# Half of the softmax tiles of an attention block transposed by VectorE and a DRAM round trip, with all engines in source order

## The chip, the core and the metric

The kernel runs on one core of a Trainium2 chip. Five engines work beside each other, each in its own instruction order: TensorE (PE, matmuls; weight loads are listed apart as PEld), VectorE (DVE), ScalarE (ACT), GpSimd (POOL) and SyncE (SP), whose work here is to issue transfers. ScalarE issues transfers too. The metric is the device time of one execution in microseconds, as the median of several runs.

## What is computed

One encoder layer for 512 positions of width 2048. The parts that matter here:

```python
h = rms_norm(x) * (1 + scale) + shift            # scale, shift, gate from silu(c) @ w_cond
aq, ak, av, ag, gq, gk, gv, gg, lr_f, lr_b = split(h @ w_in)
for window, dilation in ((128, 1), (512, 4), (2048, 16)):     # 16 heads x 64
    s = q @ k.T / 8 + bias(relative position);  mask outside the dilated window
    o_p, lse_p = softmax(s) @ v, logsumexp(s)
att = sum_p softmax_p(lse_p) * o_p
a_out = att * silu(ag)                            # attention branch
g_out = rms_norm(gla_fwd + gla_bwd) * gain * silu(gg)   # gated linear attention branch, 4 heads
out = rms_norm(x + gate * (concat(a_out, g_out) @ w_out)) * final_gain
```

The three window patterns together are one softmax over all 512 keys, with a bias row per head that holds the relative bias, the logarithm of how many patterns contain a distance, and a large number where none does. The kernel computes it so: P is 512 x 512 per head.

## The kernel before

All matrix products of the projections run as three products of rounded parts (high x high, low x high, high x low; function `three`), in fp32r. A weight of a projection comes from DRAM as a "raw" tile (4 buffers), ScalarE rounds it to its high part (`split_hi`), VectorE subtracts to get the low part (`split_lo`).

The program has three parts. The first computes the modulation, the normalised input `h` and the first two projection groups (`sa`: values, `sb`: GLA queries and the queries and keys of head pairs 0 and 1); its order on all engines is made by a planner with costs (`_plan`). The middle part is a row of "units" in a fixed order: qk2, qk4, qk6 (queries and keys of two head pairs each), gk, gv0, gv1, ag0, ag1, gg0, gg1. The last part is the output projection, o0 to o3.

A unit (function `unit`) has 8 groups of two 128-row blocks of `h`, and four output tiles in PSUM ("pj", 5 buffers, so the next unit has one buffer free and needs the others evicted). For each group it goes over the four tiles; for each tile over two blocks; each block is three matmuls, called a tick here: 64 ticks in a unit. Beside it a list of side work with positions between 0 and 1 is emitted as the ticks go by; positions of 1 and more spill into the next unit. TensorE keeps the order of the source throughout. The other engines keep it in the first part only; elsewhere the framework orders them by priorities and estimated times.

The side work of qk2, qk4, qk6 and gk is the attention of the heads whose queries and keys are ready (`attention`): 4 heads, each with 4 tiles of 128 queries, so 16 tiles in a unit and 64 in all. For each tile:

- `score`: two matmuls of queries against all 512 keys into a PSUM buffer ("pa", 3 buffers); VectorE adds the bias row and takes the minimum (line 580); ScalarE takes the exponential and its sum (583); VectorE the reciprocal (584); GpSimd scales the tile (585).
- `turn`: TensorE transposes the four 128 x 128 blocks into PSUM (597), ScalarE rounds (601), VectorE subtracts (602).
- `values`, once for each half of a head (two tiles, 256 queries): eight matmuls (611), an eviction (614) and an addition (618) into `cat`.

Queries and keys are evicted from a unit's tiles by `qk_evict`: for each head ScalarE writes rounded queries (539) and keys (548), VectorE the remainders (540, 550), and SP copies both key parts to the other 64 partitions (549, 551). These tiles and the P tiles share one pool ("t2", 16 buffers).

Sums that have nothing to do with attention (`some_sums`, 48 of them, each a 512 KB load into a raw buffer and a multiply-and-add on VectorE) are spread over the units by `SUMS_IN`; the rest goes to gg1. The 4 heads of GLA (`gla_head`) run in gv1, ag0, ag1 and gg0. The low-rank gate weights are loaded and split between gk and gv0 and used by TensorE within gv0 (`lr_tick`).

## Time and profile before

| What | Value |
|---|---|
| median of three runs | 962.89 us (958.9, 962.89, 962.98) |
| the profiled execution | 959.9 us, its span 957.9 us |
| mean granted TensorE clock | 0.997 |
| busy: PE, DVE, ACT, POOL | 939.7, 605.3, 431.5, 81.1 us |
| moved by DMA | 163.76 MB, mean 171 GB/s |
| start of qk2, qk4, qk6, gk, gv0 | 191.9, 257.3, 323.7, 390.3, 457.5 us |

A row of the profile's group table names the line, the engine, the operation, what it writes and reads with shapes and count, then the busy time and the mean duration of one in nanoseconds, then the engine's idle time before such instructions and who ended it. A row of a table of windows is a stretch of the span with its length and the busy time of each engine (and the count of instructions) in it, then the granted clock, the DMA share and GB/s. A row of a timeline is start, duration, engine, line, operation, tiles. A row of the transfers ends with the size and the median microseconds from issue to landing. Matmuls are pipelined, so a matmul's duration is longer than the step from one to the next.

### The profile page before, as it was taken

The numbers are of one execution on the slowest core, as the hardware profiler recorded it, in microseconds if no ns is written. First come the engines' busy times: TensorE is split into PE (matmuls) and PEld (weight loads), VectorE is DVE, ScalarE is ACT, GpSimd is POOL, SyncE is SP. The second block draws the span as 40 slices with busy tenths as digits, with TensorE's granted clock in tenths as the row PEclk, the third lists the DMA queues.
The fourth block names the chain that finished last, engine by engine and source line by source line (L and its number), as shares of the span: only waits on it lengthen the run. The fifth ranks groups of instructions, "written<-read, shape, count | busy, mean of one in ns | idle before, by whom it ended". The sixth has DMA issues, their size and how long they took to land.

```text
span 957.9 us, 11999 instructions
## 1 busy us (share of the span) xinstructions
PE 939.7 (98%) x4464; PEld 777.1 (81%) x4464; DVE 605.3 (63%) x900; ACT 431.5 (45%) x719; POOL 81.1 (8%) x100
## 2 busy tenths in 40 slices
PE   8999999999999999999999999999999999999996
PEld 5888788888888888888778888888887888888884
DVE  7988899675756676766435656675964352546421
ACT  5443533565655655655215544543834152233222
POOL 0000000012122022122000000000010000202120
PEclk9999999999999999999999999999999999999998
DMA  9999687443333463533454244354555464244013
GB/s 330 413 411 365 229 296 275 150 131 105 112 103 105 144 200 108 173 127 103 150 176 146 86 132 154 132 176 154 173 195 183 132 221 154 92 151 152 23 55 121
DMA packets 45180, 163.76 MB, mean 171 GB/s; under 512 B 5730, under 2 KB 6018, under 8 KB 40386
## 3 DMA queue, kind: packets, MB, share of 16 engines
q1 hardware_dynamic: 44946, 162.68, 49.9%
q8 instruction: 35, 0.57, 0.2%
q10 hardware_dynamic: 176, 0.33, 0.1%
q14 instruction: 23, 0.18, 0.1%
HBM read 154.51 MB, written 4.28 MB: 166 GB/s over the span
## 4 chain that ended last, share of the span: by engine, by line
PE 84%; DMA 6%; DVE 5%; issue 3%; ACT 1%; SPq 0%; POOL 0%; ACTq 0%; DVEq 0%; POOLq 0%
PE ps_o L170 6%; PE ps_o L169 6%; PE ps_o L171 6%; DMA rawg<-in_wg 6%; PE ps_qk L170 5%; PE ps_qk L169 5%; PE ps_qk L171 5%; PE o L611 3%; PE sta L169 3%; PE sta L170 3%; PE sta L171 3%; PE stb L171 3%; PE stb L169 3%; PE stb L170 3%; PE ps_gv L171 3%; PE ps_gv L170 3%
## 5 line engine op out<-in xcount | busy, mean ns | idle before, releaser
L585 POOL TENSOR_SCALAR p<-p,st 128x512 f32<-128x512 f32 x64 | 45.5, 711 | 406.6 <-DVE st L584 357.9
L244 DVE CUSTOM_DVE_ANT_0 cb<-cb,sb,c_bcond 128x2048 f32<-128x2048 f32 (+1 forms) x32 | 73.4, 2294 | 0.0
L583 ACT ACTIVATE p<-p,st 128x512 f32<-128x512 f32 x64 | 46.1, 721 | 56.8 <-DVE st L580 56.3
L602 DVE TENSOR_TENSOR pt<-t,pt 128x512 fp32r<-128x512 f32 x64 | 44.0, 689 | 16.2 <-ACT pt L601 15.8
L580 DVE CUSTOM_DVE_ANT_0 p<-s,g 128x512 f32<-128x512 f32 x64 | 43.6, 687 | 14.8 <-PE s L577 14.5
L601 ACT ACTIVATE pt<-t 128x512 fp32r<-128x512 f32 x64 | 37.8, 592 | 10.2 <-PE t L597 9.2
L244 DVE CUSTOM_DVE_ANT_0 rawg<-rawg,sb,gate 128x1024 f32<-128x1024 f32 x16 | 20.5, 1283 | 29.6 <-DMA rawg<-in_wg 29.6
L611 PEld LDWEIGHTS o<-pt,vv 128*128 128x128 f32 x256 | 34.7, 188 | 5.0 <-DVE pt L602 2.2
L597 PEld LDWEIGHTS t<-c_ident,p 128*128 128x128 f32 x256 | 31.8, 140 | 8.5
L597 PE MATMUL t<-c_ident,p 128*128 128x128 f32 x256 | 38.3, 272 | 0.0
L611 PE MATMUL o<-pt,vv 128*128 128x256 f32 x256 | 36.6, 283 | 0.9 <-DVE pt L602 0.8
L244 DVE CUSTOM_DVE_ANT_0 rawg<-rawg,sb,c_bcond 128x1024 f32<-128x1024 f32 x16 | 20.5, 1283 | 26.3 <-DMA rawg<-in_wg 26.3
L1014 POOL TENSOR_TENSOR x<-x,fgain 128x512 f32<-128x512 f32 x12 | 20.3, 1696 | 185.3 <-ACT ysq L1012 185.3
L1012 ACT ACTIVATE ysq<-x 128x512 f32<-128x512 f32 x16 | 10.1, 632 | 47.2 <-DVE x L1010 47.2
L767 POOL TENSOR_SCALAR dc<-st,sc 128x256 f32<-128x256 f32 x16 | 10.4, 652 | 245.5 <-DVE st L764 240.6
L1009 DVE TENSOR_TENSOR y<-ps_o,sb 128x512 f32<-128x512 f32 x16 | 10.9, 684 | 25.9 <-PE ps_o L171 25.9
L584 DVE RECIPROCAL st<-st 128x1 f32<-128x1 f32 x64 | 10.3, 162 | 24.9 <-ACT p L583 24.9
L576 PE MATMUL s<-ks,qs 128*128 128x512 f32 x64 | 25.1, 391 | 0.0
L577 PE MATMUL s<-kl,qs 128*128 128x512 f32 x64 | 25.0, 391 | 0.0
L774 ACT ACTIVATE sq<-st,sc 128x256 f32<-128x256 f32 x24 | 12.2, 509 | 26.8 <-DVE st L769 14.3
L1010 DVE TENSOR_TENSOR x<-y,x 128x512 f32<-128x512 f32 x16 | 18.0, 1125 | 0.3
L614 ACT ACTIVATE oh<-o 64x256 f32<-64x256 f32 x32 | 12.2, 382 | 13.0 <-PE o L611 12.2
(1275 smaller groups left out, 2916.7 us busy)
## 6 DMA issues: line engine op xcount, KB each, us to landing
cb<-in_wm SPq DMA_DIRECT2D x31, 1024.0 KB, 7.9
rawg<-in_wg SPq DMA_DIRECT2D x32, 512.0 KB, 3.4
raw_o<-in_w_o SPq DMA_DIRECT2D x32, 512.0 KB, 3.4
raw_qk<-in_w_qk SPq DMA_DIRECT2D x24, 512.0 KB, 3.4
rawb<-in_w_sb SPq DMA_DIRECT2D x16, 512.0 KB, 4.8
rawv<-in_wv SPq DMA_DIRECT2D x16, 512.0 KB, 3.8
raw_gv<-in_w_gv SPq DMA_DIRECT2D x16, 512.0 KB, 3.5
raw_ag<-in_w_ag SPq DMA_DIRECT2D x16, 512.0 KB, 3.3
```

What stands on the lines that cost most here:

```text
L169: mm(ps, lh, rh, start=first, stop=False)
L170: mm(ps, ll, rh, start=False, stop=False)
L171: mm(ps, lh, rl, start=False, stop=last)
L244: nc.vector.tensor_tensor_reduce(out=w, in0=w, in1=with_, op0=ALU.mult, op1=ALU.add, scale=1.0, scalar=init, accum_out=dst)
L576: mm(ps, qs[:, q], ks, start=True, stop=False)
L580: nc.vector.tensor_tensor_reduce(out=t, in0=ps, in1=gt[h][:, P * i:P * i + 512], op0=ALU.add, op1=ALU.min, scale=1.0, scalar=3e38, accum_o ...
L583: act(t, t, AF.Exp, bias=st[:, 0:1], scale=-1.0, accum_out=st[:, 1:2])
L585: nc.gpsimd.tensor_scalar(t, t, st[:, 2:3], 1.0, op0=ALU.mult, op1=ALU.mult)
L597: nc.tensor.transpose(pk[:, kt * P:kt * P + P], t[:, kt * P:kt * P + P], ident)
L601: act(hi, src, AF.Copy)
L602: tt(lo, src, hi.bitcast(F32), op=ALU.subtract)
L611: mm(po[:, :256], vv[h // 4][:, kt, h % 4, :], t[:, w, kt, :], start=kt == 0 and w == 0, stop=kt == 3 and w == 1)
```

## The change

Of each head, the tiles of the first half (`BY_DVE = (0,)`, 32 of 64 tiles) are no longer transposed by TensorE. VectorE transposes 32 x 32 blocks within the tile and orders them (`turn`), SP writes the result to DRAM (`leave`, 256 KB), and when both tiles of the half are there four transfers bring it back so that the partition is the key within a 128-block (`back`, four times 128 KB in pieces of 512 bytes). ScalarE then rounds both tiles in one instruction (`part_hi`) and VectorE subtracts (`part_lo`). The other half keeps TensorE's transposes (`pe_turn`). Each piece has a position: tile number plus an offset, in steps of 0.057 of a unit from 0.12 on. The scaling is a piece of its own, 0.75 steps behind its score, but at 15.4 steps for the last tile, which is still within the unit, so ahead of `qk_evict`.

From the end of the first part to the end of gv0, all engines but TensorE too are now in the order of the source. In qk4, qk6 and gk the first two groups of weights are one step, with 4 ticks for each tile; a unit of queries and keys splits one group more of the next unit's weights at its end. Weight loads of qk and gk units and the bias rows are issued by ScalarE. The sums leave qk6 and gk (gv0 9 to 12, gv1 2 to 5, ag0 7 to 8, gg1 4 to 5). The shift row moves from 0.05 to 0.6 of qk6; the low-rank weights are loaded and split within gk.

```diff
@@ -70,12 +70,16 @@
-ATT_AT = (0.17, 0.8, 0.04, 0.05, 0.05)
+ATT_AT = (0.12, 0.057)
+BY_DVE = (0,)
+BACK_AT = (2.7, 4.1, 4.4, 5.6)
...
-SUMS_IN = {"qk6": 4, "gk": 4, "gv0": 9, "gv1": 2, "ag0": 7, "ag1": 9, "gg0": 9}
+SUMS_IN = {"gv0": 12, "gv1": 5, "ag0": 8, "ag1": 9, "gg0": 9}
...
 def _plan(tasks, free, ready):
@@ -283,7 +287,8 @@
         if i < len(groups) and i not in raws:
             u, g = groups[i]
             raws[i] = RAW(f"raw_{u}{g}", [2, 512])
-            nc.sync.dma_start(raws[i], a["w_" + u][g])
+            queue = nc.scalar if u[:2] in ("qk", "gk") and i > 2 else nc.sync
+            queue.dma_start(raws[i], a["w_" + u][g])
@@ -535,39 +540,31 @@
-            qs = T2(f"qs{p}{j}", F32R)
+            qs, ks, kl = [T2(f"{n}{p}{j}", F32R) for n in ("qs", "ks", "kl")]
             act(qs[own], psq[own, ::-1], AF.Copy, scale=-0.125)
+            act(ks[own], psk[own], AF.Copy)
             stt(qs[oth], psq[own, ::-1], -0.125, qs[own].bitcast(F32),
                 op0=ALU.mult, op1=ALU.subtract)
-            stacks[2 * p + j] = [qs, None, None, own]
-        for j in range(2):
-            own = slice(64 * j, 64 * j + 64)
-            oth = slice(64 - 64 * j, 128 - 64 * j)
-            ks = T2(f"ks{p}{j}", F32R)
-            kl = T2(f"kl{p}{j}", F32R)
-            act(ks[own], psk[own], AF.Copy)
-            nc.sync.dma_start(ks[oth].bitcast(F32), ks[own].bitcast(F32))
             tt(kl[own], psk[own], ks[own].bitcast(F32), op=ALU.subtract)
-            nc.sync.dma_start(kl[oth].bitcast(F32), kl[own].bitcast(F32))
-            stacks[2 * p + j][1:3] = ks, kl
+            for t in (ks, kl):
+                nc.sync.dma_start(t[oth].bitcast(F32), t[own].bitcast(F32))
+            stacks[2 * p + j] = [qs, ks, kl, own]
...
         def g_load(h):
             g = gp.tile([P, 896], F32, tag="g", name=f"g{h}")
-            nc.sync.dma_start(g, bass.AP(grow.tensor, grow.offset + h * 1024, [[1, P], [1, 896]]))
+            nc.scalar.dma_start(g, bass.AP(grow.tensor, grow.offset + h * 1024, [[1, P], [1, 896]]))
...
         def score(h, i):
...
-                if h % 8 == 0 and i == 0:
-                    cat[h // 8] = B8(f"cat{h // 8}", [4, 512])
@@ -581,12 +578,20 @@
+                pr_[h, i] = t, st
+            return go
+        def scale(h, i):
+            def go():
+                t, st = pr_.pop((h, i))
                 nc.vector.reciprocal(st[:, 2:3], st[:, 1:2])
                 nc.gpsimd.tensor_scalar(t, t, st[:, 2:3], 1.0, op0=ALU.mult, op1=ALU.mult)
                 pr_[h, i] = t
             return go
-        def turn(h, i):
@@ -595,15 +600,58 @@
                 pk = PA(f"t{h}{i}")
                 for kt in range(4):
                     nc.tensor.transpose(pk[:, kt * P:kt * P + P], t[:, kt * P:kt * P + P], ident)
...
+        def turn(h, i):
+            def go():
+                t = T2(f"pt{h}{i}")
+                nc.vector.transpose(t.rearrange("p (b k r) -> p k b r", b=4, k=4), pr_.pop((h, i)))
+                pr_[h, i] = t
+            return go
+        def leave(h, i):
+            def go():
+                half, ii = divmod(i, 2)
+                if ii == 0:
+                    away[h, half] = dp.tile([2, P, 512], F32, tag=f"away{h}{half}", name=f"away{h}{half}")
+                nc.sync.dma_start(away[h, half][ii], pr_.pop((h, i)))
+            return go
+        def back(h, half):
+            def go():
+                t = away.pop((h, half))
+                f = RAW(f"pf{h}{half}", [8, 128])
+                for b in range(4):
+                    nc.sync.dma_start(f[32 * b:32 * b + 32], bass.AP(
+                        t.tensor, t.offset + P * b, [[512, 32], [32 * 512, 8], [1, P]]))
+                pf[h, half] = f
+            return go
+        def part_hi(h, half):
+            def go():
+                t = pt[h, half] = B8(f"pt{h}{half}", [2, 4, 256], F32R)
+                src = pf[h, half].rearrange("p b (k r) -> p k b r", k=4)
+                act(t[:, 0].rearrange("p k (b r) -> p k b r", b=8), src, AF.Copy)
+            return go
+        def part_lo(h, half):
+            def go():
+                src = pf.pop((h, half)).rearrange("p b (k r) -> p k b r", k=4)
+                hi, lo = [pt[h, half][:, e].rearrange("p k (b r) -> p k b r", b=8) for e in range(2)]
+                tt(lo, src, hi.bitcast(F32), op=ALU.subtract)
+            return go
         def values(h, half):
             def go():
+                if cat[h // 8] is None:
+                    cat[h // 8] = B8(f"cat{h // 8}", [4, 512])
@@ -620,20 +668,25 @@
         n = len(tiles)
-        for x in range(n + 4):
-            if x < n:
-                items.append(score(*tiles[x]))
-            if 2 <= x <= n + 1:
-                items.append(turn(*tiles[x - 2]))
-            if 3 <= x <= n + 2 and tiles[x - 3][1] % 2 == 1:
-                items.append(values(tiles[x - 3][0], tiles[x - 3][1] // 2))
+        for x in range(n):
+            h, i = tiles[x]
+            items.append((x, score(h, i)))
+            items.append((min(x + 0.75, n - 0.6), scale(h, i)))
+            half, ii = divmod(i, 2)
+            if half in BY_DVE:
+                items.append((x + 1.1, turn(h, i)))
+                items.append((x + 1.5, leave(h, i)))
+                if ii:
+                    for at, piece in zip(BACK_AT, (back, part_hi, part_lo, values)):
+                        items.append((x + at, piece(h, half)))
+            else:
+                items.append((x + 1.8, pe_turn(h, i)))
+                if ii:
+                    items.append((x + 3.2, values(h, half)))
+        items.sort(key=lambda v: v[0])
         g_load(heads[0])
...
+        start, step = ATT_AT
+        return [(start + step * x, go) for x, go in items]
@@ -846,39 +899,49 @@
         side = [x for x in side if x[0] < 1]
         ps = [PJ(f"ps_{name}_{i}") for i in tiles]
         pos, tick, ticks = 0, 0, 16 * len(tiles)
-        for q in range(KT // 2):
-            g = gorder[q] if name == "o3" else q
-            i0 = gi[name, g]
+        order_ = gorder if name == "o3" else list(range(KT // 2))
+        steps = [order_[:2]] if name in ("qk4", "qk6", "gk") else [order_[:1], order_[1:2]]
+        for step in steps + [[g] for g in order_[2:]]:
             todo = []
             if 0 in tiles:
...
+                end = upto[name, step[-1]] + (name[:2] == "qk" and step[-1] == order_[-1])
+                todo = list(range(gi[name, order_[0]], end + 1))
+                if len(step) == 1:
+                    for i in todo:
+                        split_hi(i)
+                    for ahead in (1, 2):
+                        fetch(end + ahead)
+            for g in step:
+                split_lo(gi[name, g])
             for n, i in enumerate(tiles):
...
+                for g in step:
+                    hi, lo = wts[gi[name, g]]
+                    for kk in range(2):
+                        k = 2 * g + kk
+                        rh, rl = (h_hi[:, k, :], h_lo[:, k, :]) if rhs is None else rhs[k]
+                        first, last = (g, kk) == (order_[0], 0), (g, kk) == (order_[-1], 1)
...
+                        tick += 1
+                        if len(step) == 2 and tick == 8:
+                            split_hi(end)
+                            for ahead in (1, 2):
+                                fetch(end + ahead)
+                        if tick == 10 if len(step) == 2 else tick % (2 * len(tiles)) == 2:
+                            for i_ in todo:
+                                if i_ <= upto[name, step[-1]]:
+                                    split_lo(i_)
+                        while pos < len(side) and side[pos][0] * ticks <= tick:
+                            urgent(side[pos][1])
+                            pos += 1
+                    if lr is not None:
+                        lr(4 * g + i)
@@ -897,34 +960,47 @@
-    for p in range(2):
-        qk_evict(p, psb["b", 4 + 2 * p], psb["b", 5 + 2 * p])
-    for n, p in (("qk2", 0), ("qk4", 2), ("qk6", 4)):
-        ps = unit(n, False, attention((p, p + 1)) + ([(0.05, shift_row)] + some_sums(n) if p == 4 else []))
-        for q in range(2):
-            qk_evict(p + 2 + q, ps[2 * q], ps[2 * q + 1])
...
+    with tc.manual_schedule(engines=PLANNED):
+        side = attention((0, 1))
+        for i in range(3):
+            fetch(i)
+        split(0)
+        for p in range(2):
+            qk_evict(p, psb["b", 4 + 2 * p], psb["b", 5 + 2 * p])
+        for n, p in (("qk2", 0), ("qk4", 2), ("qk6", 4)):
+            ps = unit(n, False, side + ([(0.6, shift_row)] if p == 4 else []))
+            side = attention((p + 2, p + 3))
+            for q in range(2):
+                qk_evict(p + 2 + q, ps[2 * q], ps[2 * q + 1])
...
+        ps = unit("gk", False, side + [(0.7, lr_load), (0.85, lambda: lr_part(0)), (0.9, lambda: lr_part(1))])
...
+        ps = unit("gv0", True, some_sums("gv0"), lr=lr_tick)
     gla["v0"] = B8("gv0", [4, 512])
     for i in range(4):
         act(gla["v0"][:, i, :], ps[i], AF.Copy)
```

82 lines of the change are left out of this document (29 added, 53 removed).

## The prediction

> **What bounds the kernel now.** I read the page's first lines, then the table of windows with one row for each unit of the middle part, then TensorE's own waits.
>
> ```profile
> span 957.9 us, 11999 instructions
> ...
> PE 939.7 (98%) x4464; PEld 777.1 (81%) x4464; DVE 605.3 (63%) x900; ACT 431.5 (45%) x719; POOL 81.1 (8%) x100
> ```
> ```profile
> core 0: us, PE busy (x) PEld busy (x) DVE busy (x) ACT busy (x) POOL busy (x), PEclk, DMA share, GB/s
> 191.90:257.30 65.40, 65.37 (x346) 54.89 (x345) 43.50 (x90) 38.81 (x75) 11.15 (x16) 1.00 0.37 113
> 257.30:323.70 66.40, 66.37 (x353) 55.90 (x352) 41.93 (x89) 37.43 (x72) 11.17 (x16) 1.00 0.36 108
> 323.70:390.30 66.60, 66.57 (x355) 55.89 (x354) 47.24 (x100) 37.60 (x73) 11.13 (x16) 1.00 0.51 162
> 390.30:457.50 67.20, 66.36 (x353) 55.91 (x352) 44.98 (x94) 36.50 (x70) 12.05 (x16) 1.00 0.42 132
> 457.50:510.40 52.90, 52.52 (x234) 41.21 (x233) 20.16 (x26) 12.16 (x15) 0.00 (x0) 1.00 0.46 150
> 510.40:564.60 54.20, 54.20 (x272) 45.91 (x271) 32.97 (x44) 27.05 (x47) 1.93 (x4) 1.00 0.39 128
> 564.60:618.70 54.10, 54.10 (x271) 45.86 (x270) 35.22 (x48) 25.47 (x43) 1.93 (x4) 1.00 0.44 143
> ```
> ```profile
> PE o L611 <- DVE pt L602: 0.8, 1, 0.8
> ...
> PE plr L924 <- DVE lrs L917: 0.4, 1, 0.4
> ```
>
> TensorE is busy for 98% of the span. In the units qk2, qk4 and qk6 (the first three windows) it is never free: 65.37 of 65.40 us, 66.37 of 66.40, 66.57 of 66.60, at a granted clock of 1.00. The other engines all have room there (VectorE 43.5 of 65.4 us). So in these units time is only won by taking matmuls away, and only lost where a new wait reaches TensorE. The fourth window (gk) and the fifth (gv0) hold the only waits near the change, 0.8 and 0.4 us, both for VectorE. The execution that I sum against took 959.9 us around its span of 957.9; the three timed runs are 958.9, 962.89 and 962.98, on both sides of it, so I add nothing for them.
>
> **What the change takes off TensorE.** 32 of the 64 P tiles lose their four transposes (line 597). The chain of waits prices a group and a product as TensorE spends them, and the timeline shows the step of an ordinary matmul.
>
> ```profile
> 204.27 0.44 PE t L597 x4
> ...
> 210.68 0.94 PE o L611 x8
> ```
> ```profile
> 202.97 0.39 PE L576 MATMUL s<-ks,qs 128*128 128x512 f32 x1
> 203.20 0.39 PE L577 MATMUL s<-kl,qs 128*128 128x512 f32 x1
> 203.42 0.39 PE L169 MATMUL ps_qk<-h_hi,qk21h 128*128 128x512 f32 x1
> ```
>
> A group of four costs 0.44 us (the pipelined loss behind it included). 32 x 0.44 = 14.1 us less. The rest of TensorE's work is the same; the first step of qk4, qk6 and gk only orders it otherwise (two groups of weights for one output tile, then the next tile). The matmul step is 0.23 us, so a "tick" of three is 0.69, a score of two 0.46, a product 0.94. The waits in gk and gv0 go, too: gk loses its four sums, and the split of the low-rank weights moves from the end of gk into it. That is 1.2 us less.
>
> **What it adds, and where that hides.** The rows nearest to the new instructions:
>
> ```profile
> L585 POOL TENSOR_SCALAR p<-p,st 128x512 f32<-128x512 f32 x64 | 45.5, 711 | 406.6 <-DVE st L584 357.9
> ...
> L602 DVE TENSOR_TENSOR pt<-t,pt 128x512 fp32r<-128x512 f32 x64 | 44.0, 689 | 16.2 <-ACT pt L601 15.8
> ...
> L601 ACT ACTIVATE pt<-t 128x512 fp32r<-128x512 f32 x64 | 37.8, 592 | 10.2 <-PE t L597 9.2
> ```
> ```profile
> L313 ACT ACTIVATE c_h<-raw_o 128x1024 fp32r<-128x1024 f32 x4 | 4.2, 1057 | 3.7 <-DMA raw_o<-in_w_o 3.7
> L297 DVE TENSOR_TENSOR c_l<-raw_o,c_h 128x1024 fp32r<-128x1024 f32 x4 | 4.9, 1220 | 1.3 <-ACT c_h L313 1.3
> L717 DVE TENSOR_TENSOR_SCAN b<-rst,g 128x512 f32<-128x512 f32 x4 | 4.9, 1225 | 0.1
> L244 DVE CUSTOM_DVE_ANT_0 rawv<-rawv,shb,vbias 128x1024 f32<-128x1024 f32 x8 | 10.3, 1282 | 12.0 <-DMA rawv<-in_wv 12.0
> L540 DVE SCALAR_TENSOR_TENSOR qs<-ps_qk,qs 64x512 fp32r<-64x512 f32 x12 | 8.3, 689 | 0.4
> L550 DVE TENSOR_TENSOR kl<-ps_qk,ks 64x512 fp32r<-64x512 f32 x12 | 8.3, 689 | 0.9 <-ACT ks L548 0.6
> ```
>
> In a unit, VectorE loses 8 subtractions of 0.689 (5.5 us) and gets 8 turns and 4 subtractions of double width (4 x 1.22 = 4.9). No row shows a turn. An ordinary 128x512 pass takes 0.689, the dearest one-pass row of that size, the scan, 1.225; since a turn reads and writes each element once I take 0.69 and keep 1.23. In qk2 that gives 43.5 - 5.5 + 5.5 + 4.9 = 48.4 us (52.7 with the dear turn) in a unit of some 61.9 (65.4 less 8 x 0.44): 78 to 85%. TensorE's matmuls cover it; without cover, the surplus beyond 61.9 would be the price, and that needs a turn of 2.4 us. A turn waits for GpSimd's scaling (0.71) with the next tile's bias-and-minimum ahead of it; 8 x 0.71 at most, inside the same 13 us that VectorE has over. ScalarE trades 8 x 0.592 for 4 x 1.057, nothing. The shift row's two transfers move from 0.05 to 0.6 of qk6; behind them on SP stand ways out and back, which have three steps (11 us) to the product, and its readers are now in gv0: 0. The eight sums of 1.28 us that leave qk6 and gk go to gv0 (3), gv1 (3), ag0 (1) and gg1 (1); VectorE rises from 20.2 to 24.0 in 52.9 us, from 33.0 to 36.8 in 54.2, from 35.2 to 36.5 in 54.1, each under matmuls. If such a sum were uncovered it would cost its 1.28. The bounds are 0 and 8 x 1.28 = 10.2; with 15 us and more free in each I take 0.
>
> Weight loads of these units and the bias tiles are issued by ScalarE instead of SP: 12 in a unit. One such issue is in this trace:
>
> ```profile
> 509.90 1.06 ACT L313 ACTIVATE gv12h<-raw_gv 128x1024 fp32r<-128x1024 f32 x1 [0.54 <-PE ps_gv L170]
> 510.60 0.92 ACTq L946 DMA_DIRECT2D rst<-in_rst  x1
> 510.87 0.58 ACT L930 ACTIVATE gv<-ps_gv 128x512 f32<-128x512 f32 x1
> ```
>
> ScalarE went on computing beside it (two activations overlap the 0.92 us). Their waits for a raw buffer come last from the subtraction that frees it, which stands earlier in the source than anything queued behind them, so I put them at 0; bound 12 x 0.92 on an engine that has 26 us free.
>
> **The seam, where the change costs.** With source's order on every engine I can follow the passage from one of these units into the next, three times (qk2 to qk4, qk4 to qk6, qk6 to gk), with T the first matmul of the new unit. The old unit's last head has tiles 12 to 15; 13 closes the half that goes through DRAM. Its way back stands at 15.7 steps, 0.12 + 0.057 x 15.7 = 1.015: it spills into the new unit, and so into SP's queue behind the eight copies of key parts that the splits of queries and keys issue. Its rounding (17.1 steps) stands ahead of the first exponential of the new unit on ScalarE, its rest (17.4) ahead of that unit's first bias-and-minimum on VectorE (line 580), and TensorE's product of it (18.6 steps, tick 12) needs both the rest and one of three "pa" buffers, all held by then by results that wait in VectorE's queue behind that rest.
>
> ```profile
> 203.63 0.69 DVE L580 CUSTOM_DVE_ANT_0 p<-s,g 128x512 f32<-128x512 f32 x1 [0.54 <-PE s L577]
> ```
> ```profile
> 266.26 0.69 DVE L580 CUSTOM_DVE_ANT_0 p<-s,g 128x512 f32<-128x512 f32 x1
> ...
> 267.84 0.16 DVE L584 RECIPROCAL st<-st 128x1 f32<-128x1 f32 x1 [0.27 <-ACT p L583]
> ```
> ```profile
> 250.22 0.33 SPq L564 DMA_DIRECT2D g<-grow  x1
> ...
> 255.74 0.47 SPq L551 DMA_DIRECT2D kl<-kl  x1
> ```
> ```profile
> raw_o<-in_w_o SPq DMA_DIRECT2D x32, 512.0 KB, 3.4
> ...
> g<-grow SPq DMA_DIRECT2D x16, 448.0 KB, 4.4
> ...
> x<-in_x SPq DMA_DIRECT2D x4, 1024.0 KB, 6.8
> out<-x SPq DMA_DIRECT2D x16, 256.0 KB, 2.6
> ks<-ks SPq DMA_DIRECT2D x16, 128.0 KB, 2.2
> ...
> c_maskf<-in_maskf SPq DMA_DIRECT2D x1, 64.0 KB, 3.2
> ```
>
> The last score (tick 63) ends 0.5 us before T: its last matmul starts 0.92 ahead (0.23 and a tick) and takes 0.39; VectorE starts 0.04 after (203.59 to 203.63). From there to the end of the reciprocal are 1.74 us (266.26 to 268.00): T+1.3. That reciprocal is the "last scaling" which now stands ahead of the splits: VectorE waits some 0.9 us for the exponential, with all the splits queued behind it. Then the rest of the next weights, 1.22: T+2.5. Eight splits of queries and keys at 0.69 and a gap of 0.03: T+8.3. SP issues the last copy (0.47): T+8.8. Four ways back at 0.33 and 0.04: the last is issued at T+9.9. A load from DRAM of 64 KB lands in 3.2 us here, a copy within the core in 2.2, 448 KB in 4.4; the piece has 128 KB from DRAM, so I take 3.2: T+13.1. Rounding 1.06, rest 1.22, bias-and-minimum 0.69 and 0.08: T+16.2 with the hand-overs.
>
> TensorE would be at that product after 12 ticks (8.3), two groups of transposes (0.9), two scores (0.9) and a product (0.9): T+11.0. It also meets an earlier wait: output tile 1 of the new unit needs the bank of the first query tile, free after three splits (T+4.6), at T+3.2 (four ticks, one group); these 1.4 us lie inside the later one. So a seam costs 16.2 - 11.0 = 5.2 us, three 15.6. By the bounds of the landing alone (2.2 to 4.4): 12.6 to 19.2.
>
> The Trainium skill bears on that landing ("DMA: Bandwidth & Descriptors", section "Anatomy of one DMA — SWDGE (gpsimd) path"): it fits a transfer as 2.0 us and bytes at 436 GB/s, for transfers that GpSimd issues; an estimate from that is 2.3 us for 128 KB, a seam of 4.3 us and a total of 957.5. The trace's 3.2 us for half the bytes is above it, and I keep the row.
>
> Sum: 959.9 - 14.1 - 1.2 + 15.6 = 960.2.
>
> **The rivals.**
> 1. *The way back is not late* (948.8 us). The turn of tile 13 stands at tick 60, some 2.7 us before T; its way out takes 2.6 (the row of out). If SP can issue the way back at once, the last piece lands near T+5, its rest follows the splits on VectorE (T+8.3, two subtractions, T+9.7, 10.9), and only output tile 1's wait stays: 3 x 1.4 = 4.2, 959.9 - 14.1 - 1.2 + 4.2 = 948.8. For it: the source leaves 1.4 steps (some 5 us) between way back and rounding, and the seams of before have no wait at all. Against it: the queue's order as read above; the way back would have to pass eight copies.
> 2. *The way back is slow* (971). One place: the last of the four pieces of tile 13. It comes in rows of 512 bytes and shares the rings with weight loads of 512 KB. Each us over 3.2 goes straight through rounding, rest and bias-and-minimum to TensorE, three times; from 4.8 us on, the sum is over the half per cent (960.2 + 3 x 1.6 = 965.0). At 6.8 us, the row of the 1 MB loads of x, it is 960.2 + 3 x 3.6 = 971.0. For it: 4.4 us for 448 KB, 3.4 for one weight load alone. Against it: the DMA share of 0.37 in qk2, and 3.2 us for the small load. Within a unit the same delay has cover: from the way back to the product lie 2.9 steps, some 10 us.
> 3. *The transposes are not worth 0.44*: if only the four starts went (the pipelined loss staying), a third less would come off: 965. The matmul behind them is short again where nothing transposes (203.42 on), so I give it no chance of its own; it is inside the range.
>
> **How the numbers follow.** Chances: the seam as worked out 0.44 (960.2, own range 957 to 964 by the landing), rival 1 0.38, rival 2 0.18. The predicted time is that of the first, 960. The range reaches from rival 1, with a few us below it where tile 1's bank comes free in time (959.9 - 14.1 - 1.2 = 944.6), to near rival 2: 944 to 970. What can be told from no change is half a per cent, 4.8 us. Rival 1 is faster throughout; of the first case, about a fifth (short landing, or less ahead of it); rival 2 mostly slower: faster 0.46, same 0.37, slower 0.17.
>
> **What would show it.** Right: 128 transposes in place of 256; qk2 at some 61.9 us, and qk4, qk6 and gk each near 68 (66.4 - 3.5 + 5.2); TensorE idle some 5 us at the start of qk4, qk6 and gk, ended by VectorE's bias-and-minimum or rest, ScalarE idle before the rounding of tile 13's half, ended by a DMA; SP's way back issued after the last copy of key parts. Wrong: no such idle time and four units of about 62 us (rival 1); landings over 5 us (rival 2); TensorE idle in the middle of the units, or in gv0 to gg0 beyond what is there now, which would mean that VectorE's fill or the moved sums, put at nothing, decide.

## The result, and the profile after

The changed kernel takes 974.45 us (median of four runs, 972.29 to 975.87); the kernel before, over its four runs, 960.89 (956.95 to 962.98). The ratio is 1.016, with a 95% interval of 1.0135 to 1.0184: slower by 1.6%. The prediction was 960, with 944 to 970 for the range, so it missed, by 14 us and on the slow side. The execution profiled after took 975.03 us around a span of 973.2, at a mean granted clock of 0.992 (before: 0.997).

Line numbers have moved: the bias-and-minimum is now line 577, the exponential 580, the reciprocal 588, GpSimd's scaling 589, TensorE's transposes 602, VectorE's turn 614, the way out 623 and back 632, its rounding 641 and its rest 648, the product 659, the splits of queries and keys 544 to 548 and the copies 550, the rest of a weight 302.

First the same table of windows as before: qk2, qk4, qk6, gk, gv0, gv1. Behind the length of a window stand the busy times of PE, PEld, DVE, ACT and POOL.

```profile
192.60:252.20 59.60, 59.60 (x297) 49.99 (x296) 38.72 (x80) 30.98 (x59) 9.71 (x14) 1.00 0.60 179
252.20:324.60 72.40, 65.19 (x321) 53.72 (x320) 45.65 (x93) 36.52 (x69) 11.98 (x16) 0.98 0.54 159
324.60:395.80 71.20, 65.43 (x323) 53.75 (x322) 45.29 (x92) 36.26 (x68) 11.99 (x16) 0.98 0.60 171
395.80:467.00 71.20, 65.13 (x321) 53.68 (x320) 45.94 (x95) 36.03 (x69) 11.98 (x16) 0.98 0.53 156
467.00:524.00 57.00, 54.89 (x250) 43.07 (x249) 29.96 (x44) 17.70 (x25) 1.38 (x2) 1.00 0.67 225
524.00:580.60 56.60, 54.37 (x272) 45.79 (x271) 37.11 (x50) 26.63 (x47) 1.91 (x4) 1.00 0.46 147
```

qk2 is the unit that was hoped for: 59.60 us instead of 65.40, TensorE never free. (61.9 was foreseen; some products now fall into the next unit: 297 matmul records against 346, of which 32 are the transposes. At the other end of the row gv0 has 250 against 234.) The other five are longer than before (66.40, 66.60, 67.20, 52.90 and 54.20), because TensorE stands in them: 72.40 - 65.19 = 7.2 us in qk4, 5.8 in qk6, 6.1 in gk, 2.1 in gv0, 2.2 in gv1. Over the six windows the time rises from 372.7 to 388.0 us, 15.3, which is the whole growth of the span. TensorE's idle time in them rises from 1.3 to 23.4 us (+22.1), and its busy time falls only from 371.4 to 364.6 (-6.8).

TensorE's own waits, by who ended them (total, times, longest):

```profile
PE o L659 <- DVE st L577: 12.9, 3, 5.2
PE kt L798 <- DVE ki L788: 2.2, 1, 2.2
PE ps_qk L173 <- DVE qs L546: 1.5, 2, 0.7
PE t L602 <- POOL p L589: 1.4, 3, 0.7
...
PE ps_gk L174 <- DVE gk1l L302: 1.1, 1, 1.1
PE ps_qk L174 <- DVE qk41l L302: 1.0, 1, 1.0
```

Three long ones stand before a product and are ended by the bias-and-minimum; around each lie shorter ones, for the rest of the second group's weights (1.0 at the first seam, 1.1 at the third), for a bank that the splits of queries and keys hold (0.7) and for a scaling of GpSimd. Here is the first seam, from the timeline (start, duration, engine; in brackets the idle time before it and who ended it). The first matmul of qk4 starts at 252.23, so T is 252.23:

```profile
252.71 0.14 DVE L588 RECIPROCAL st<-st 128x1 f32<-128x1 f32 x1
...
254.38 0.17 DVE L588 RECIPROCAL st<-st 128x1 f32<-128x1 f32 x1 [0.93 <-ACT p L580]
254.46 1.21 DVE L302 TENSOR_TENSOR qk41l<-raw_qk,qk41h 128x1024 fp32r<-128x1024 f32 x1
...
255.72 0.50 PE L174 MATMUL ps_qk<-h_hi,qk41l 128*128 128x512 f32 x1 [1.04 <-DVE qk41l L302]
...
257.87 0.50 PE L173 MATMUL ps_qk<-h_hi,qk40h 128*128 128x512 f32 x1 [0.73 <-DVE qs L546]
...
259.25 1.80 SPq L550 DMA_DIRECT2D ks<-ks  x1
...
260.73 0.69 DVE L548 TENSOR_TENSOR kl<-ps_qk,ks 64x512 fp32r<-64x512 f32 x1
...
262.79 0.46 SPq L550 DMA_DIRECT2D kl<-kl  x1
263.30 2.08 SPq L632 DMA_DIRECT2D pf<-away  x4
268.16 1.06 ACT L641 ACTIVATE pt<-pf 128x1024 fp32r<-128x1024 f32 x1 [6.45 <-DMA pf<-away]
269.25 1.23 DVE L648 TENSOR_TENSOR pt<-pf,pt 128x1024 fp32r<-128x1024 f32 x1 [6.50 <-ACT pt L641]
270.39 0.68 DVE L577 CUSTOM_DVE_ANT_0 p<-s,g 128x512 f32<-128x512 f32 x1
...
271.23 2.04 PE L659 MATMUL o<-pt,vv 128*128 128x256 f32 x8 [5.25 <-DVE st L577]
```

That is the predicted chain, link by link: reciprocal, rest of the next weights, eight splits, the last copy on SP, the four ways back, rounding on ScalarE, rest and bias-and-minimum on VectorE, product on TensorE. Only the product does not run at its old pace: eight matmuls in 2.04 us, where the chain of waits of before had 0.94 for them. The next table of windows shows why: it cuts the time from 264.20 on into stretches of 3.41 us, and the column behind POOL is the granted clock.

```profile
264.20:267.62 3.42, 1.78 (x11) 1.21 (x9) 0.00 (x0) 0.00 (x0) 0.00 (x0) 1.00 0.66 172
267.62:271.03 3.41, 0.00 (x0) 0.00 (x0) 1.78 (x4) 2.00 (x2) 0.00 (x0) 1.00 0.46 154
271.03:274.45 3.42, 3.22 (x12) 2.96 (x13) 2.36 (x7) 2.04 (x6) 0.69 (x1) 0.50 0.34 134
274.45:277.86 3.41, 3.41 (x17) 2.81 (x16) 2.50 (x6) 0.88 (x3) 0.69 (x1) 1.00 0.20 77
...
410.98:414.39 3.41, 0.59 (x5) 0.62 (x6) 2.57 (x4) 2.46 (x4) 0.00 (x0) 1.00 0.46 154
414.39:417.80 3.41, 3.41 (x13) 2.83 (x12) 2.05 (x7) 1.58 (x6) 0.69 (x1) 0.50 0.39 135
```

After a stretch in which TensorE did nothing (0.00) the clock is 0.50 for 3.4 us, and then 1.00 again. The same happens behind the other two long waits (last two rows: the third), although TensorE was still busy for 0.80 and 0.59 us of the stretches before. TensorE was busy for nearly all of each slow stretch, so an estimate of what they cost is half of 3.41 us, three times: 5.1 us.

The new operations themselves, from the groups and the transfers, and what is left of TensorE's transposes:

```profile
L614 DVE STREAM_TRANSPOSE pt<-p 128x512 f32<-128x512 f32 x32 | 22.7, 709 | 4.3 <-POOL p L589 4.2
L641 ACT ACTIVATE pt<-pf 128x1024 fp32r<-128x1024 f32 x16 | 16.8, 1048 | 21.6 <-DMA pf<-away 21.6
...
L602 PE MATMUL t<-c_ident,p 128*128 128x128 f32 x128 | 19.6, 275 | 1.5 <-POOL p L589 1.4
```
```profile
pf<-away SPq DMA_DIRECT2D x64, 128.0 KB, 3.1
```

### The profile page after: what moved, and what is told of

The parts are those of the page before. It is cut to its first block, busy times and chain, and to the rows that moved or that the text cites. A ratio compares the mean times of both kernels' runs of the same rounds, so it can differ in the third digit from the quotient of the medians.

```text
span 973.2 us, 11851 instructions
## 1 busy us (share of the span) xinstructions
PE 933.2 (96%) x4336; PEld 767.9 (79%) x4336; DVE 620.7 (64%) x917; ACT 426.7 (44%) x704; POOL 82.6 (8%) x100
## 4 chain that ended last, share of the span: by engine, by line
PE 35%; DVE 9%; DMA 8%; ACT 5%; issue 4%; SPq 0%; POOL 0%; ACTq 0%; DVEq 0%; POOLq 0%
PE ps_o L173 6%; PE ps_o L174 6%; PE ps_o L175 6%; DMA rawg<-in_wg 4%; DMA rawv<-in_wv 2%; PE ps_gg L174 2%; PE ps_gg L173 2%; PE ps_gg L175 2%; PE ps_ag L175 2%; PE ps_ag L173 2%; PE ps_ag L174 2%; PE ps_gv L174 1%; PE ps_gv L173 1%; PE ps_gv L175 1%; DVE rawg L248 1%
## 5 line engine op out<-in xcount | busy, mean ns | idle before, releaser
L659 PE MATMUL o<-pt,vv 128*128 128x256 f32 x256 | 37.8, 291 | 13.9 <-DVE st L577 12.9
L659 PEld LDWEIGHTS o<-pt,vv 128*128 128x128 f32 x256 | 35.8, 196 | 18.0 <-issue 14.2
L648 DVE TENSOR_TENSOR pt<-pf,pt 128x1024 fp32r<-128x1024 f32 x16 | 19.6, 1226 | 31.4 <-ACT pt L641 31.4
L606 DVE TENSOR_TENSOR pt<-t,pt 128x512 fp32r<-128x512 f32 x32 | 21.7, 685 | 7.5 <-ACT pt L605 7.4
L641 ACT ACTIVATE pt<-pf 128x1024 fp32r<-128x1024 f32 x16 | 16.8, 1048 | 21.6 <-DMA pf<-away 21.6
L614 DVE STREAM_TRANSPOSE pt<-p 128x512 f32<-128x512 f32 x32 | 22.7, 709 | 4.3 <-POOL p L589 4.2
L827 ACT ACTIVATE sq<-st,sc 128x256 f32<-128x256 f32 x24 | 12.2, 509 | 27.3 <-DVE st L817 13.7
L666 DVE TENSOR_TENSOR cat<-o,oh 64x256 f32<-64x256 f32 x32 | 13.4, 417 | 14.0 <-ACT oh L662 13.8
L588 DVE RECIPROCAL st<-st 128x1 f32<-128x1 f32 x64 | 10.0, 156 | 18.9 <-ACT p L580 18.7
L602 PEld LDWEIGHTS t<-c_ident,p 128*128 128x128 f32 x128 | 15.2, 140 | 7.7 <-POOL p L589 5.0
```

The costliest lines, as they stand in the source:

```text
L606: tt(lo, src, hi.bitcast(F32), op=ALU.subtract)
L614: nc.vector.transpose(t.rearrange("p (b k r) -> p k b r", b=4, k=4), pr_.pop((h, i)))
L659: mm(po[:, :256], vv[h // 4][:, kt, h % 4, :], t[:, w, kt, :], start=kt == 0 and w == 0, stop=kt == 3 and w == 1)
```

## The experiments

Two theories were on the table once the trace was read. The first: the way back of tile 13 comes late in SP's queue, and with it the long waits and the half clock; the cure is to issue it ahead of the copies, or to ask for its product later. The rival: source's order itself costs the time, through VectorE's queue at the seam, whatever the way back does. In the runs below "the planner's order" means that VectorE, ScalarE, GpSimd and SP are ordered in the middle part by the framework's priorities, as in the kernel before. Each comparison has its own runs of the kernel before beside it (medians 956.75 to 958.11), and the ratios go by those. The result's own set had 960.89. A difference between the medians of two runs of different sets therefore carries up to 4 us that belong to the sets; where this matters, the difference is also given against each run's own median of the kernel before ("by own medians").

**The way back issued earlier.** At 15.4 steps instead of 15.7 it falls just inside the old unit (0.12 + 0.057 x 15.4 = 0.998), so ahead of the copies.

```diff
-BACK_AT = (2.7, 4.1, 4.4, 5.6)
+BACK_AT = (2.4, 4.1, 4.4, 5.6)
```

> The way back of a DRAM half is placed 2.4 instead of 2.7 steps after its tile, so at 15.4 steps, the last place within the unit and ahead of the splits of queries and keys in SP's queue. Theory (the way back is late because it stands behind the eight copies of key parts): it is issued some 8 us earlier at a seam, TensorE's waits of 5.2, 4.0 and 4.0 us at the first product of a seam go to under 1 us, and with them the three stretches of half clock (3.4 us each, 5 us in all); the waits for the first weights' rest and the first query bank stay. About 957 us (954 to 961). Rival (the transfer itself is slow, or ScalarE's and VectorE's order is the cause whatever SP does): the long waits stay, 970 to 976.

Measured: 957.0 us, ratio 0.9993 [0.9973, 1.0013]. One number gives back 17 us (15 by own medians), and the long waits are gone: from qk2 to gv0 none is over 1.1 us. So they came from the place in SP's queue. What is left are short waits, and with them a clock that still falls, twice in the profiled execution. Its ten runs go from 953.71 to 964.09 us, with mean clocks of 0.990 to 0.998, so how often it falls seems to differ from run to run. Two windows of this kernel, on both sides of the first drop:

```profile
320.49:323.90 3.41, 1.75 (x6) 1.16 (x7) 3.29 (x5) 2.29 (x5) 1.44 (x1) 1.00 1.00 264
323.90:327.31 3.41, 3.41 (x11) 2.73 (x10) 3.25 (x6) 2.79 (x7) 0.00 (x0) 0.50 1.04 206
```
The waits in the first of these stretches, from its timeline:
```profile
321.42 0.50 PE L174 MATMUL ps_qk<-h_hi,qk61l 128*128 128x512 f32 x1 [0.99 <-DVE qk61l L302]
323.58 0.54 PE L173 MATMUL ps_qk<-h_hi,qk60h 128*128 128x512 f32 x1 [0.73 <-DVE qs L546]
```

No single wait there is longer than 1.0 us; TensorE was busy for 1.75 of 3.41 us, and the next stretch has the clock at 0.50. The second drop comes at the end of qk6, where a product waits 1.1 us for the rounding and 0.9 us for the rest of what came back.

**The order alone.** Everything of the change but the turn: all 64 tiles are transposed by TensorE.

```diff
-BY_DVE = (0,)
+BY_DVE = ()
```

> No half goes through VectorE and DRAM; all 64 tiles are turned by TensorE, in source's order and with all else as in the changed kernel. Theory: TensorE gets 32 groups of transposes back (14 us), the long waits and the half clock go (13 and 5 us), the short waits at the seams and in gv0 and gv1 stay: 968 to 972, that is 7 to 11 us slower than the kernel before, which is then the price of the order and of the moved sums alone. Rival (the order costs nothing by itself, all loss hangs on the DRAM half): 959 to 963.

Measured: 965.09 us, ratio 1.008 [1.0065, 1.0095], between the two forecasts. The window of qk4:

```profile
256.00:324.30 68.30, 66.96 (x353) 55.72 (x353) 40.88 (x89) 36.95 (x72) 11.98 (x17) 1.00 0.33 104
```

qk6 and gk are 68.40 and 68.30 us; with the planner's order and the same work (last run of this section) these units are 66.30 to 66.40. So the order costs 2 us a unit without any way back, 1.3 of them as idle time of TensorE (68.30 - 66.96); the edit that I had put at nothing is worth 6.5 us in all (965.09 - 958.63; 6.0 by own medians).

**The turn alone.** The change without source's order in the middle part:

```diff
-    with tc.manual_schedule(engines=PLANNED):
+    with ExitStack():
```

> The half goes through VectorE and DRAM as in the changed kernel, but from the end of the first part to gv0 the framework orders the engines other than TensorE again, as in the kernel before. Theory: the long wait is made by source's order on SP; a planner that sees the copies wait can issue the way back ahead of them, the long waits go and the time is 946 to 958. Rival (the half's trip is too long for its place whatever the order): TensorE still waits 4 us and more at the seams, 968 to 978.

Measured: 953.88 us, ratio 0.9958 [0.9943, 0.9973]: as expected, a small gain. Of TensorE's longer waits near the change one kind is left:

```profile
PE o L659 <- DVE pt L648: 7.3, 4, 2.4
```

It is the product again, now waiting for the rest of the way back. The timeline of the first seam has three of the four ways back amid the copies of keys, and the rounding behind them:

```profile
252.41 0.47 SPq L550 DMA_DIRECT2D ks<-ks  x1
...
254.34 1.60 SPq L632 DMA_DIRECT2D pf<-away  x3
256.04 0.47 SPq L550 DMA_DIRECT2D ks<-ks  x1
...
262.50 1.06 ACT L641 ACTIVATE pt<-pf 128x1024 fp32r<-128x1024 f32 x1 [1.45 <-DMA pf<-away]
```

TensorE's clock falls twice here as well (mean 0.993).

**The rest of the second group's weights earlier**, in the old unit instead of the new one:

```diff
                             for i_ in todo:
-                                if i_ <= upto[name, step[-1]]:
-                                    split_lo(i_)
+                                split_lo(i_)
```

> VectorE subtracts the rest of the second weight group of the next unit at tick 58 instead of behind the last reciprocal. Theory: TensorE's waits for that rest (1.0, 1.0 and 1.1 us) go, the splits start 1.2 us earlier and the chain behind the way back is that much shorter: 3 to 5 us less than the changed kernel, 969 to 972; the long waits stay at 3 us and more. Rival (VectorE is simply full there and the work only changes places): within 1.5 us of the changed kernel, 973 to 976.

Measured: 974.73 us, ratio 1.0175 [1.0158, 1.0192]: no gain. The wait for that rest is gone, but the one for the bank grew (0.7 to 1.3), and the long ones stay:

```profile
PE o L659 <- DVE st L577: 12.0, 3, 4.4
...
PE ps_qk L173 <- DVE qs L546: 2.7, 2, 1.3
```

VectorE has the same splits to do whichever piece comes first; the idle time of TensorE over the whole span stays at 40 us (40.1 against 40.0), so the wait that went moved to other readers. The clock is at 0.50 for six stretches of 3.41 us in this trace, against three.

**The last scaling behind the splits**, where x + 0.75 puts it:

```diff
-            items.append((min(x + 0.75, n - 0.6), scale(h, i)))
+            items.append((x + 0.75, scale(h, i)))
```

> The changed kernel without the clause that puts a unit's last scaling ahead of the splits of the next queries and keys: reciprocal and scaling of the last tile come behind the eight splits on VectorE. Theory (the first wait of each seam is VectorE held by that reciprocal and then splitting the rest of the next weights): the wait of 1.04 us for that rest stays or falls to about 0.5 (the reciprocal no longer stands ahead of it), the wait of 0.73 us for tile 1's bank falls by up to 0.9, but the last tile's transposes on TensorE now wait for the late scaling; the reciprocal moves from T+2.2 to about T+9, its transposes are issued soon after the next unit's first tiles, so TensorE stands about 4 to 5 us at each of three seams: 978 to 988 us. Rival (the last tile's transposes stand late enough in TensorE's order that the late scaling is hidden, and only VectorE's early second is saved): 968 to 973 us, with the long waits of 4 to 5 us unchanged.

Measured: 971.02 us, ratio 1.0149 [1.0132, 1.0167]. The mechanism is the theory's and the time is the rival's:

```profile
PE t L602 <- POOL p L589: 15.0, 6, 3.7
```

TensorE does wait for the late scaling, up to 3.7 us. But while it stands there, the way back lands, and no wait before a product is left: the stall came earlier and took the place of the long one. The two stand in a row behind the same queue, so they do not add. What the clause that puts the last scaling ahead of the splits is worth isn't shown: by the medians the kernel without it is 3.4 us faster (974.45 - 971.02), by own medians it is 0.7 slower, and the intervals of the two ratios overlap. It buys TensorE's early transposes with a longer wait behind them.

**One group first again** at the start of qk4, qk6 and gk:

```diff
-        steps = [order_[:2]] if name in ("qk4", "qk6", "gk") else [order_[:1], order_[1:2]]
+        steps = [order_[:1], order_[1:2]]
```

> The changed kernel with the two-group first step of qk4, qk6 and gk taken back: each output tile gets 2 ticks before the next one, not 4. Theory (the two-group step is cover for the first waits of a seam, and the prediction was right that it adds no work of its own): TensorE asks for output tile 1's bank at T+1.4 instead of T+3.2, and VectorE frees it no earlier than about T+5, so the first waits of a seam grow from 1.8 us to about 3.5 us; but the long wait behind them shrinks by the same amount, since both end with the same queue on VectorE: 972 to 978 us, and the half clock may come earlier. Rival (the two-group step itself brings the waits, since it needs the rest of the second group's weights at once): the wait for that rest goes, 968 to 971 us.

Measured: 978.89 us, ratio 1.0218 [1.0203, 1.0234], 1 us past the theory's range. TensorE's waits:

```profile
PE ps_qk L173 <- DVE qs L546: 6.8, 2, 3.4
PE o L659 <- DVE st L577: 5.1, 3, 2.4
```

The bank's wait grows from 0.7 to 3.4 us and the product's shrinks from 4.3 to 1.7 in the mean (12.9 and 5.1 in three). So the two-group step is not a cause, and without it the kernel is 4.4 us slower (978.89 - 974.45; 7.6 by own medians). But as cover it saves no idle time: over the whole span TensorE is idle for 39.9 us without it and 40.0 with it, and busy for 937.3 against 933.2. The trace has the clock at 0.50 for six stretches of 3.41 us instead of three; three more, at 1.7 us each, are an estimated 5.1 us. By this trace, then, the step is worth something because the clock falls less often with it.

**The product later.** The planner's order as in the run of the turn alone, and the product of a turned half one tile later:

```diff
-BACK_AT = (2.7, 4.1, 4.4, 5.6)
+BACK_AT = (2.7, 4.1, 4.4, 6.6)
...
-    with tc.manual_schedule(engines=PLANNED):
+    with ExitStack():
```

> The run of the turn alone (the planner's order kept, 953.9 us) with one number changed: the product of a turned half stands one tile later (its place 5.6 becomes 6.6), so that the way back has about 3 us more. Theory (what is left at the seams there is the way back, 7.3 us of TensorE's waits in four places plus two half clocks of about 1.7 us): nearly all of it goes, 944 to 950 us. Rival (the waits at the seams come from the splits of the next weights or from banks, and the product only was the instruction that stood at them): 951 to 955 us, with the waits found at the next instruction.

Measured: 942.08 us, ratio 0.985 [0.9835, 0.9865]. It is faster than both kernels, and the gain is a little larger than expected. Its windows (first, second and last of qk2 to gv0) and the group of its products:

```profile
192.50:251.10 58.60, 58.60 (x290) 49.19 (x289) 40.26 (x83) 33.05 (x60) 10.43 (x15) 1.00 0.57 159
251.10:313.50 62.40, 62.40 (x321) 52.80 (x320) 45.20 (x93) 36.52 (x68) 13.08 (x16) 1.00 0.66 182
...
438.60:493.70 55.10, 55.10 (x258) 44.05 (x257) 28.12 (x41) 15.29 (x21) 0.70 (x1) 1.00 0.66 209
```
```profile
L659 PE MATMUL o<-pt,vv 128*128 128x256 f32 x256 | 35.7, 282 | 0.0
```

TensorE is busy without a break from qk2 to gv0, at a clock of 1.00, and the 256 matmuls of the products have 0.0 us idle before them. VectorE has as much work here (45.20 us in qk4) as in the changed kernel (45.65).

**The same, with the way back early too.**

```diff
-BACK_AT = (2.7, 4.1, 4.4, 5.6)
+BACK_AT = (2.4, 4.1, 4.4, 6.6)
...
-    with tc.manual_schedule(engines=PLANNED):
+    with ExitStack():
```

> As the run before it, and the way back issued 0.3 of a tile earlier (its place 2.7 becomes 2.4). Theory (once the product is late the way back is not what comes last): the same as the run before it within 2 us, 943 to 950 us. Rival (the way back still comes last, by its landing beside the copies of the keys): 2 to 4 us below the run before it.

Measured: 945.54 us (941.66 to 947.65), ratio 0.989 [0.9873, 0.9906]: no gain over the run before it but 0.4% more time, so the way back no longer decides there. The profiled execution shows a new wait, 1.3 us in two for copied keys, whose copies now stand behind the way back in SP's queue; whether that is all of the 3.5 us between the medians is open, since the profiled execution was itself the shortest, 941.66.

**Source's order with both**: the way back early and the product late.

```diff
-BACK_AT = (2.7, 4.1, 4.4, 5.6)
+BACK_AT = (2.4, 4.1, 4.4, 6.6)
```

> The changed kernel in its source order with the way back early (957.0 us before) and the product one tile later as well. Theory (with the way back early the seams wait for the splits and for banks, 1.0 and 0.7 us each, and not for the product): no more than 1 to 3 us are gained, 953 to 957 us. Rival (the product's wait is still hidden in it): 946 to 951 us, as with the planner's order.

Measured: 951.81 us, ratio 0.9955 [0.9939, 0.997]: between the two forecasts, 5.2 us better than with the way back early alone (3.8 by own medians). Its windows of qk4 and gk:

```profile
251.30:316.00 64.70, 63.35 (x321) 52.68 (x321) 45.56 (x93) 36.23 (x68) 11.97 (x16) 1.00 0.60 176
...
380.80:446.40 65.60, 63.51 (x322) 52.71 (x321) 46.36 (x95) 35.98 (x71) 11.94 (x16) 1.00 0.58 170
```

The clock is 1.00 throughout these units; by estimate that is 3.4 us (two drops of 1.7 in the profiled run with the way back early alone), most of the gain. The short waits stay: these units are 64.70 and 65.60 us long, against 62.40 and 62.50 with the planner's order. Against the planner's order with the late product, source's order still loses 6 to 10 us (951.81 against 945.54 and 942.08).

**The planner's order, TensorE's transposes**: the fastest run without its turn.

```diff
-BY_DVE = (0,)
-BACK_AT = (2.7, 4.1, 4.4, 5.6)
+BY_DVE = ()
+BACK_AT = (2.7, 4.1, 4.4, 6.6)
...
-    with tc.manual_schedule(engines=PLANNED):
+    with ExitStack():
```

> The fastest run so far (942.1 us: turn by VectorE, planner's order, late product) with all tiles transposed by TensorE again. Theory (the turn is worth its 14.1 us where nothing of it is late, and the other moved things are worth nothing): 955 to 958 us. Rival (a part of the fast run's gain comes from the moved sums, loads and scaling): 949 to 953 us.

`BACK_AT` has no effect here, since no half comes back. Measured: 958.63 us, ratio 1.0005 [0.9996, 1.0015], 0.6 us past the theory's range: the kernel before. So the moved sums, loads and scaling gain nothing on their own, and the turn, where nothing of it is late, is worth 16.5 us (958.63 - 942.08; 15.6 by own medians). In gv1 a wait is found here too (first row; the others are the windows of qk4 and gk that the comparisons above use):

```profile
PE kt L798 <- DVE ki L788: 2.1, 1, 2.1
```
```profile
256.70:323.00 66.30, 66.30 (x354) 55.93 (x353) 41.28 (x89) 37.76 (x72) 11.07 (x16) 1.00 0.36 108
...
389.40:455.70 66.30, 66.30 (x354) 55.92 (x353) 43.21 (x93) 39.02 (x75) 11.11 (x16) 1.00 0.40 121
```

The kernel before had no such wait (54.20 us busy of 54.20 in gv1). It comes with what the change moved besides the turn, and it is 0.3 to 2.8 us long in the other traces; the three more sums that VectorE has in gv1 would fit, but they were not tried apart.

The four corners, in us, with the ratio to each run's own kernel before:

| | TensorE transposes all | VectorE turns half |
|---|---|---|
| planner's order | 958.63 (1.0005) | 953.88 (0.9958); product later 942.08 (0.985) |
| source's order | 965.09 (1.008) | 974.45 (1.016); way back early 957.0 (0.9993); and product later 951.81 (0.9955) |

## Why the prediction was wrong

**What held.** The bound, the place and the mechanism. TensorE sets the time; the transposes come off; the greater part of the loss lies at the three seams and is the way back behind eight copies (15 to 17 us come back with it). 128 transposes are left. The turn takes 709 ns (I took 0.69 and kept 1.23), the rounding 1048, the rest 1226, the landing 3.1 us in the median where I took 3.2: rival 2, the slow landing, did not happen. Rival 1 did not either, but the run with one number changed shows how near it was: 0.3 of a step puts the way back on the other side of the copies, and 957.0 us is closer to its 948.8 than to the result. The transfers that ScalarE issues cost nothing that TensorE's waits show.

**Which steps failed.** Over the six windows I had TensorE's idle time at +14.4 (15.6 - 1.2) and its busy time at -14.1. Measured are +22.1 and -6.8. So 7.7 us were missed in idle time and 7.3 in busy time, and together they are the error of 15.0 within these windows. By size: the half clock 5.1, the waits in gv0 and gv1 4.3, the waits at the three seams 3.5, and 2.2 of busy time that were not taken apart. The half clock alone, a term that the sum left out, is more than the 4.5 us by which the result lies above the range.

| Term of the sum | predicted | measured |
|---|---|---|
| idle in qk4, qk6, gk | 3 x 5.2 = 15.6 | 7.2 + 5.8 + 6.1 = 19.1 |
| idle in gv0 (0.4 before) | 0 | 2.1 |
| idle in gv1 (0 before) | 0 | 2.2 |
| half clock | not seen | 3 x 1.7 = 5.1 |
| transposes | -14.1 | -15 to -16.5, where nothing is late |

1. *"These 1.4 us lie inside the later one."* This is the wrong step of the seam. A wait ahead of the long one would lie inside it if it held up TensorE alone. But both ends of the long wait moved. TensorE stood 1.04 and 0.73 us on the way (the first, for the rest of the second group's weights, is not in the prediction at all) and arrived at the product at 265.98, T+13.7, not T+11.0. The chain came later, too: the reciprocal ended at T+2.3 (254.55) instead of T+1.3, since the one before it had started at 252.71, behind an addition to `cat` that waited for ScalarE; the last copy was issued by T+11.0 instead of T+8.8; the four ways back took 2.08 us instead of 4 x 0.37; the bias-and-minimum ended at T+18.9 instead of T+16.2. The difference at this seam came out as 5.25, almost the predicted 5.2, with both sides 2.7 us late; TensorE lost the 2.7 as well. That this one number fits is luck. VectorE was about 1 us behind here when the unit began, which I had left out, and one copy's issue held SP for 1.80 us (259.25) where those of the other two seams took 0.46 to 0.55. In those seams the bias-and-minimum ended at T+17.2 and T+17.9, TensorE came to the product at T+13.5 and T+14.2, and the long waits were 3.9 and 3.8; their idle time in all is still 5.8 and 6.1 us, because the short waits come on top.

2. *The clock was not in the sum.* I had a wait of 5 us in the forecast and read 1.00 in every window of before, where no wait was long. What it does when TensorE stands is now in the rows: 0.50 for 3.4 us behind each of the long waits, of which only the first filled a whole stretch. The Trainium skill has this ("TensorE: Matmul & The Clock Gate", section "Part 1: The HAM clock gate (the "warmup" mystery)"): a free-running window of 3413 ns, and half the clock after one idle window. The 0.50 and the length agree with this trace. By that page, an estimate, up to 3 x 1.7 = 5.1 us would have belonged on my sum, some 965, since a wait of 5.2 us can hold one whole window; I left it out.

3. *Edits put at nothing.* Source's order was "only" an order: alone it costs 6.5 us, and with the transposes still on TensorE that shows as 68.3 us instead of 66.3 a unit. The moved sums were at 0 between 0 and 10.2; with them comes a wait of 2.1 to 2.2 us in gv1. The gain of 1.2 us in gk and gv0 did not come: gv0 stands 2.1 us instead of 0.4, and with the planner's order and the late product it doesn't stand (55.10 us busy of 55.10), which points to the order. TensorE idle in gv0 and gv1 is one of the prediction's own signs of being wrong.

4. *0.44 a group was about a tenth too little.* The windows of qk4 with the planner's order, 66.30 and 62.40 us, give 3.9 for eight groups, 0.49 each (0.48 by the windows of qk6 and gk); rival 3, which had them cheaper, falls with that. This error made the forecast too slow, not too fast.

The upper end of the range was rival 2, a landing that takes longer; what came were terms that stood in no case at all. Of the 7.3 us of busy time, the half clock explains an estimated 5.1; the slower restart of a matmul behind each wait (0.50 us instead of 0.39 at 255.72 and 257.87) goes the same way, and the rest was not taken apart.

**Where the gain went.** Where nothing is late the turn gives some 15 to 16.5 us. From that state (942.08) the changed kernel (974.45) is 32.4 us away (28.2 by own medians), and the runs lead back in three steps: source's order 9.7 (with the way back moved ahead of the copies so that it isn't late, 951.81), the product asked for a tile earlier 5.2 (957.0; 3.8 by own medians), and the way back behind the copies 17.4 (974.45; 14.7 by own medians). The first step changes two things at once, but the way back's place alone was worth no gain in the planner's order.

## What to carry to other kernels

When a producer leaves an engine through a queue, ask at which place in that queue its transfer stands once the unit ends, and let the consumer ask for it a step later before making anything faster: here one number was worth 15 to 17 us in one order (the place of the way back) and 10 to 12 in the other (the place of the product, 953.88 to 942.08), where everything that the turn takes off TensorE is 15 to 16.5. An order written in source's sequence carried the lag of one engine into the others here, so its price has to be read where two units meet, not from the sum of busy times. And a wait of TensorE is not its length alone: add the half clock behind it, as soon as roughly half of a 3.4 us stretch is idle (in the traces here always where TensorE was busy for 1.36 us of 3.41 or less at the full clock, never from 1.82 on).

## What the runs showed that I had not expected

The clock falls behind sums of short waits as well. In the run with the way back early no wait in the stretch from 320.49 was above 1.0 us, yet with 1.75 us busy of 3.41 the next stretch ran at 0.50. In the changed kernel the stretch from 264.20 had 1.78 us busy and the clock stayed at 1.00 in the next. Over the traces kept, stretches between 1.46 and 1.78 us went both ways: in the run with one group first again, one with 1.46 us busy was followed by 0.50 and one with 1.47 by 1.00. So the limit seems to lie near half of a stretch, whatever the longest wait in it; since the ends of matmuls are modelled, it was not fixed more closely. A stretch that itself ran at 0.50 needed more to get back: with 2.17 us busy (from 269.18 in the run with the second group's rest earlier) the next one was at 0.50 again, with 3.22 (from 271.03 in the changed kernel) at 1.00. The Trainium skill's advice on the page named above (section "Why this matters for your kernels") is to have no idle gaps of over some 3 us; taken as the whole rule, it would have the full clock behind the stretch from 320.49, and the measurement says otherwise.

The time of the transfers back goes with the order. In the changed kernel they take 3.1 us in the median, and 3.0 to 3.5 in the other runs of source's order; with the turn alone in the planner's order, amid copies, the median is the following:

```profile
pf<-away SPq DMA_DIRECT2D x64, 128.0 KB, 4.5
```

With the late product in that order they take 4.9 and 4.5 us, and yet no product waits. So the planner's order alone did not remove the seam's wait, and a later product did. What makes the transfers longer there was not tried apart.
